# Softmax times V on one core: four heads loaded ahead in a fixed queue order, and a loop of 24 passes in place of the unrolled program

## The chip, the cores and the metric

The kernel runs on one core of a Trainium2 chip. The metric is the device time of one execution in microseconds (us), lower is better. A core has five engines that run their own instruction streams and meet through semaphores: TensorE (PE, with its weight loads shown apart as PEld), VectorE (DVE), ScalarE (ACT), GpSimd (POOL) and SyncE (SP). Here SP only issues DMA transfers. A transfer is spread over 16 DMA engines, and all that SP issues stands in one queue (q1 in the profile).

## The reference

```python
"scores": np.random.randn(8, 12, 1024, 1024).astype(np.float32)
"v":      np.random.randn(8, 12, 1024, 64).astype(np.float32)

scores_max = np.max(scores, axis=-1, keepdims=True)
attn = np.exp(scores - scores_max)
attn = attn / (np.sum(attn, axis=-1, keepdims=True) + 1e-8)
return np.matmul(attn, v).astype(np.float32)
```

So there are 96 independent heads. Each has a 1024x1024 matrix of scores (4 MB), a softmax along its rows, and a product with a 1024x64 matrix v (256 KB), which gives a 1024x64 output (256 KB).

## The kernel before

The kernel handles the 96 heads one after the other. A head's 1024 query rows lie on 128 partitions, R = 8 rows on each: row r of partition p is query p*8 + r. Per head n it does this:

- SP issues the load of v (L100, 128x512 fp32) and that of the scores (L104, one transfer of 4 MB, 128x8192 fp32; for the last head alone four transfers of 1 MB). POOL converts v to fp16 beside a column of ones (`vones`, L107).
- For each r, ACT takes the exponential of two rows at a time (EB = 2, L113, four calls a head) from `s_nat` to `p_nat` in fp16. No maximum is subtracted. PE transposes the row's eight 128x128 blocks into `psT` (L117, eight weight loads and eight matmuls), and DVE copies `psT` to `pt` (L123).
- Two rows later (LAG = 2), `finish` multiplies `pt` with `vones` (L76, eight weight loads and eight matmuls, 65 columns: 64 of v and the sum of the row). After every four rows (G = 4) DVE takes the reciprocal of the sums (L87) and multiplies (L88) into `out_sb`. After the eighth row SP issues the head's store (L95).

The whole program is unrolled: PE alone has 24576 instructions, SP 288 transfers and waits. Buffers come from rotating pools (4 for the scores, 4 for v, 3 for the outputs, 5 for `psT`, 3 for `psO`). A scheduler decides the order on each engine from the order in which the code is written and from when a pool's buffer comes free. SP works strictly in its order: while one of its instructions waits, all behind it wait. Each transfer raises one of eight completion semaphores (DMAHW0 to DMAHW7, taken in turn), and a transfer also waits for the one that used its semaphore before, eight transfers back.

Of the kernel before, what the change touches and what calls it, by code (L numbers as in the profile page):

```python
# [1 line left out]

# [5 lines left out]

FP32 = mybir.dt.float32
FP16 = mybir.dt.float16  # L10
EXP = mybir.ActivationFunctionType.Exp


@with_exitstack
def kernel(
    ctx: ExitStack,
    tc: tile.TileContext,
    scores: bass.AP,
    v: bass.AP,
    out: bass.AP,  # L20
):
    nc = tc.nc
    P = 128

    B, H, SQ, SK = scores.shape
    Bv, Hv, SKv, D = v.shape
    assert (B, H, SK) == (Bv, Hv, SKv)
    BH = B * H
    assert SQ % P == 0 and SK % P == 0
    R = SQ // P  # L30
    C = SK // P
    M = D + 1
    EB = 2
    G = 4
    LAG = 2
    NV = 3

    sc_bh = scores.rearrange("b h (p r) j -> (b h) p r j", p=P)  # L40
    v_bh = v.rearrange("b h (p c) d -> (b h) p c d", p=P)
    out_bh = out.rearrange("b h (p r) d -> (b h) p r d", p=P)

    const_pool = ctx.enter_context(tc.tile_pool(name="const", bufs=1))
    s_pool = ctx.enter_context(tc.tile_pool(name="spool", bufs=4))
    p_pool = ctx.enter_context(tc.tile_pool(name="ppool", bufs=6))
    v_pool = ctx.enter_context(tc.tile_pool(name="vpool", bufs=4))
    pt_pool = ctx.enter_context(tc.tile_pool(name="ptpool", bufs=5))
    ob_pool = ctx.enter_context(tc.tile_pool(name="obpool", bufs=3))
    rc_pool = ctx.enter_context(tc.tile_pool(name="rcpool", bufs=4))  # L50
    psT_pool = ctx.enter_context(tc.tile_pool(name="psTp", bufs=5, space=bass.MemoryType.PSUM))
    psO_pool = ctx.enter_context(tc.tile_pool(name="psOp", bufs=3, space=bass.MemoryType.PSUM))

    ident32 = const_pool.tile([P, P], FP32, name="ident32")
    make_identity(nc, ident32)
    ident16 = const_pool.tile([P, P], FP16, name="ident16")
    nc.vector.tensor_copy(out=ident16[:], in_=ident32[:])  # L57


    vones_bufs = []  # L60
    for k in range(NV):
        vo = const_pool.tile([P, C, M], FP16, name=f"vones{k}")
        nc.vector.memset(vo[:, :, D : D + 1], 1.0)  # L63
        vones_bufs.append(vo)

    pending = []

    def finish(u):

        n, r, pt, st = u  # L70
        g = r % G
        if g == 0:
            st["psO"] = psO_pool.tile([P, G, M], FP32, tag="psO", name="psO")
        psO = st["psO"]
        for c in range(C):
            nc.tensor.matmul(  # L76
                out=psO[:, g, :],
                lhsT=pt[:, c * P : (c + 1) * P],
                rhs=st["vones"][:, c, :],
                start=(c == 0),  # L80
                stop=(c == C - 1),
            )
        if g == G - 1:
            if r == G - 1:
                st["out_sb"] = ob_pool.tile([P, R, D], FP32, tag="out_sb", name="out_sb")
            recip = rc_pool.tile([P, G, 1], FP32, tag="recip", name="recip")
            nc.vector.reciprocal(out=recip[:], in_=psO[:, :, D : D + 1])  # L87
            nc.vector.tensor_tensor(  # L88
                out=st["out_sb"][:, r - G + 1 : r + 1, :],
                in0=psO[:, :, 0:D],  # L90
                in1=recip[:].to_broadcast([P, G, D]),
                op=mybir.AluOpType.mult,
            )
        if r == R - 1:
            nc.sync.dma_start(out=out_bh[n], in_=st["out_sb"][:])  # L95

    for n in range(BH):
        last = n == BH - 1
        v_sb = v_pool.tile([P, C, D], FP32, tag="v_sb", name="v_sb")
        nc.sync.dma_start(out=v_sb[:], in_=v_bh[n])  # L100
        s_nat = s_pool.tile([P, R, SK], FP32, tag="s_nat", name="s_nat")
        step = EB if last else R
        for r in range(0, R, step):
            nc.sync.dma_start(out=s_nat[:, r : r + step, :], in_=sc_bh[n, :, r : r + step, :])  # L104

        vones = vones_bufs[n % NV]
        nc.gpsimd.tensor_copy(out=vones[:, :, 0:D], in_=v_sb[:])  # L107
        st = dict(vones=vones)

        for r in range(R):  # L110
            if r % EB == 0:
                p_nat = p_pool.tile([P, EB, SK], FP16, tag="p_nat", name="p_nat")
                nc.scalar.activation(out=p_nat[:], in_=s_nat[:, r : r + EB, :], func=EXP)  # L113
            p_row = p_nat[:, r % EB, :].rearrange("p (q c) -> p c q", c=C)
            psT = psT_pool.tile([P, SK], FP16, tag="psT", name="psT")
            for c in range(C):
                nc.tensor.transpose(  # L117
                    out=psT[:, c * P : (c + 1) * P],
                    in_=p_row[:, c, :],
                    identity=ident16[:],  # L120
                )
            pt = pt_pool.tile([P, SK], FP16, tag="pt", name="pt")
            nc.vector.tensor_copy(out=pt[:], in_=psT[:])  # L123
            pending.append((n, r, pt, st))
            if len(pending) > LAG:
                finish(pending.pop(0))
    while pending:
        finish(pending.pop(0))


# [1 line left out]
_INS = ['scores', 'v']  # L132
_OUTS = [((8, 12, 1024, 64), 'float32')]


# [23 lines left out]
```

## Time and profile before

| | |
|---|---|
| median of 17 runs | 1287.81 us (1283.03 to 1293.08) |
| the profiled execution | 1285.99 us |
| its span in the profile | 1284.2 us, so 1.8 us lie around it |
| instructions | 27588 |
| bytes moved by the kernel's queue | 453.00 MB |
| mean rate over the span | 354 GB/s |
| mean granted clock of TensorE | 0.763 |

The page gives for each engine the time that it was busy, then the span in 40 slices, the DMA queues, the chain of work that ended last, and the groups of instructions by line. In a table of stretches the columns are the stretch, its length, the busy time of PE, PEld, DVE, ACT and POOL with their instruction counts, the granted TensorE clock, the mean busy share of the 16 DMA engines, and the rate in GB/s. A DMA share above 1 means that packets overlapped on an engine. "SPq" is SP issuing transfers. A line of the waits names who waited, for whom, and then the sum in us, the number of waits and the longest one.

### The profile page before, as it was taken

What the parts mean: (1) busy time and instruction counts of PE and PEld (TensorE: products, weight loads), DVE (VectorE), ACT (ScalarE), POOL (GpSimd) and SP (SyncE); (2) the same over time, 40 slices, a digit from 0 to 9 for tenths busy, and PEclk for the clock granted to TensorE, in tenths of its full rate; (3) what the DMA queues carried; (4) which work ended last, traced back from release to release, by engine and by line L of the source; (5) the groups of instructions that cost most, each with busy time, mean ns of one, the idle gap of its engine ahead of it and who ended that gap; (6) DMA issues with size and microseconds to landing.
All of it is one profiled execution on the core that took longest, in us unless ns stands there. A gap on an engine that the chain in (4) does not pass through costs nothing.

```text
span 1284.2 us, 27588 instructions
## 1 busy us (share of the span) xinstructions
PE 801.2 (62%) x12288; PEld 763.4 (59%) x12288; DVE 619.5 (48%) x1156; ACT 704.8 (55%) x385; POOL 59.9 (5%) x102
## 2 busy tenths in 40 slices
PE   4666566665756666566665666656656665766657
PEld 4566566654656666566664656656556664656556
DVE  3445454454544544445453554545445454454545
ACT  4464565645646565465644655455555645646455
POOL 0000000000000000000000000000000000000000
PEclk9777777777777877777777777777777777777778
DMA  9898898888988889998988989989798898988986
GB/s 400 329 357 361 345 373 335 362 359 346 367 359 352 355 343 362 355 365 344 361 360 345 377 335 357 374 361 374 309 372 356 352 369 350 366 340 354 377 345 263
DMA packets 42023, 454.76 MB, mean 354 GB/s; under 512 B 4656, under 2 KB 4656, under 8 KB 29232
## 3 DMA queue, kind: packets, MB, share of 16 engines
q1 hardware_dynamic: 41904, 453.00, 87.9%
q8 instruction: 96, 1.57, 0.5%
q14 instruction: 23, 0.19, 0.0%
HBM read 427.82 MB, written 25.17 MB: 353 GB/s over the span
## 4 chain that ended last, share of the span: by engine, by line
DMA 54%; PE 21%; ACT 8%; DVE 8%; issue 6%; SPq 3%; ACTq 0%
DMA s_nat<-in_scores_dram 54%; PE psT L117 16%; ACT p_nat L113 8%; PE psO L76 5%; DVE pt L123 3%; DVE out_sb L88 3%; SPq L100 2%; DVE recip L87 1%; SPq L95 1%; SPq L104 0%; ACTq L113 0%
## 5 line engine op out<-in xcount | busy, mean ns | idle before, releaser
L113 ACT ACTIVATE p_nat<-s_nat 128x2048 f16<-128x2048 f32 x384 | 703.5, 1903 | 572.1 <-DMA s_nat<-in_scores_dram 556.8
L117 PE MATMUL psT<-ident,p_nat 128*128 128x128 f16 x6144 | 636.5, 269 | 439.2 <-ACT p_nat L113 438.8
L123 DVE COPY pt<-psT 128x1024 f16<-128x1024 f16 x768 | 528.9, 690 | 606.9 <-PE psT L117 595.1
L117 PEld LDWEIGHTS <-p_nat 128*128 128x128 f16 x6144 | 540.0, 156 | 464.7 <-ACT p_nat L113 455.3
L76 PE MATMUL psO<-vones,pt 128*128 128x65 f16 x6144 | 347.7, 206 | 39.9 <-DVE pt L123 39.9
L76 PEld LDWEIGHTS <-pt 128*128 128x128 f16 x6144 | 300.0, 108 | 52.0 <-DVE pt L123 52.0
L107 POOL CAST vones<-v_sb 128x512 f16<-128x512 f32 x96 | 59.2, 617 | 1204.3 <-DMA v_sb<-in_v_dram 1115.4
L88 DVE TENSOR_TENSOR out_sb<-psO,recip 128x256 f32<-128x256 f32 x192 | 80.6, 420 | 3.3
L87 DVE RECIPROCAL recip<-psO 128x4 f32<-128x4 f32 x192 | 34.1, 178 | 50.1 <-PE psO L76 50.1
L113 ACT ACT_TABLE_LOAD x1 | 1.3, 1283 | 0.7 <-PEq L143 0.7
L63 DVE MEMSET vones<- 128x8 f16 x3 | 0.1, 65 | 0.8 <-PEq L143 0.8
L57 DVE CAST ident<-ident 128x128 f16<-128x128 f32 x1 | 0.2, 227 | 0.4 <-POOL ident masks.py:199 0.4
masks.py:199 POOL TENSOR_SCALAR_AFFINE_SELECT ident<-ident 128x128 f32<-128x128 f32 x1 | 0.3, 292 | 0.1
masks.py:197 POOL MEMSET ident<- 128x128 f32 x1 | 0.2, 204 | 0.3 <-POOLq L143 0.3
L143 POOL MEMSET const-float32-0.0<- 128x1 f32 x1 | 0.1, 98 | 0.2 <-issue 0.2
L143 POOL MEMSET const-bfloat16-1.0<- 128x1 bf16 x1 | 0.1, 101 | 0.0
L143 POOL MEMSET const-uint8-127<- 128x1 uint8 x1 | 0.1, 101 | 0.0
L143 POOL MEMSET const-float32-1.0<- 128x1 f32 x1 | 0.1, 98 | 0.0
## 6 DMA issues: line engine op xcount, KB each, us to landing
s_nat<-in_scores_dram SPq DMA_DIRECT2D x95, 4096.0 KB, 13.9
v_sb<-in_v_dram SPq DMA_DIRECT2D x96, 256.0 KB, 3.0
out_dram<-out_sb SPq DMA_DIRECT2D x96, 256.0 KB, 2.6
s_nat<-in_scores_dram SPq DMA_DIRECT2D x4, 1024.0 KB, 8.1
```

What stands on the lines that cost most here:

```text
L57: nc.vector.tensor_copy(out=ident16[:], in_=ident32[:])
L63: nc.vector.memset(vo[:, :, D : D + 1], 1.0)
L76: nc.tensor.matmul(out=psO[:, g, :], lhsT=pt[:, c * P : (c + 1) * P], rhs=st["vones"][:, c, :], start=(c == 0), stop=(c == C - 1),)
L87: nc.vector.reciprocal(out=recip[:], in_=psO[:, :, D : D + 1])
L88: nc.vector.tensor_tensor(out=st["out_sb"][:, r - G + 1 : r + 1, :], in0=psO[:, :, 0:D], in1=recip[:].to_broadcast([P, G, D]), op=mybir.Al ...
L95: nc.sync.dma_start(out=out_bh[n], in_=st["out_sb"][:])
L100: nc.sync.dma_start(out=v_sb[:], in_=v_bh[n])
L107: nc.gpsimd.tensor_copy(out=vones[:, :, 0:D], in_=v_sb[:])
L113: nc.scalar.activation(out=p_nat[:], in_=s_nat[:, r : r + EB, :], func=EXP)
L117: nc.tensor.transpose(out=psT[:, c * P : (c + 1) * P], in_=p_row[:, c, :], identity=ident16[:],)
L123: nc.vector.tensor_copy(out=pt[:], in_=psT[:])
L143: nc = _bacc.Bacc("TRN2", target_bir_lowering=False, num_devices=1)
```

## The change

Two things are changed together.

1. The order on SP's queue is written out by hand. Four buffers for the scores, four for v and four for `vones` belong to the four heads of a pass (k = 0 to 3). The first four heads are loaded before the loop. After that, the load of head n + 4 stands where head n's eighth row has been started (its exponentials release the buffer), and head n's store stands behind it. `queue` ties each transfer to the one before it on SP. The score load of every fourth head is two transfers of 2 MB, and the splitting of the last head's load into four goes.
2. `tc.For_i(0, 96, 4, iteration_sync="reg_based")` makes a loop in hardware: each engine has the code of four heads once and runs it 24 times. Waits in the loop compare with a value in a register that grows from pass to pass; there is no barrier between passes. In the last pass the loads are skipped by a condition.

Around these, all buffers are named tiles that `take` hands out in turn: 8 for `p_nat` (6 before), 4 for `pt` (5), 4 for `out_sb` (3), 4 for `psT` (5), 4 for `psO` (3). The work on the data is the same, instruction by instruction.

```diff
-    NV = 3
+    AHEAD = 4
...
+    s_bufs = buffers(sb_pool, AHEAD, [P, R, SK], FP32, "s_nat")
+    v_bufs = buffers(sb_pool, AHEAD, [P, C, D], FP32, "v_sb")
+    p_bufs = buffers(sb_pool, 8, [P, EB, SK], FP16, "p_nat")
+    pt_bufs = buffers(sb_pool, 4, [P, SK], FP16, "pt")
+    out_bufs = buffers(sb_pool, 4, [P, R, D], FP32, "out_sb")
...
+    psT_bufs = buffers(ps_pool, 4, [P, SK], FP16, "psT")
+    psO_bufs = buffers(ps_pool, 4, [P, G, M], FP32, "psO")
...
+    def queue(dma):
+        if queued:
+            tc.add_manual_dep(dma.ins, queued[-1].ins.name, ..., reason="queue order")
+        queued.append(dma)
...
         if r == R - 1:
-            nc.sync.dma_start(out=out_bh[n], in_=st["out_sb"][:])
+            dma = nc.sync.dma_start(out=one(out_bh, n), in_=st["out_sb"][:])
...
+            queue(dma)
...
+    def load(k, n, step=R, **cond):
+        queue(nc.sync.dma_start(out=v_bufs[k][:], in_=one(v_bh, n), **cond))
         for r in range(0, R, step):
...
+    def load_next(k, n0):
+        n = (n0 + (AHEAD + k)) % BH
+        load(k, n, R if k < AHEAD - 1 else R // 2, cond=n0 < BH - AHEAD)
+
+    def heads(n0):
+        for k in range(AHEAD):
...
+                nc.vector.tensor_copy(out=pt[:], in_=psT[:])
+                if r == R - 1:
+                    load_next(k, n0)
+                pending.append((n0 + k, r, pt, st))
+                if len(pending) > LAG:
+                    finish(pending.pop(0))
+        while pending:
+            finish(pending.pop(0))
...
+    for k in range(AHEAD):
+        load(k, k)
+    with tc.For_i(0, BH, AHEAD, iteration_sync="reg_based") as n0:
+        queued.clear()
+        heads(n0)
```

How the orders differ, first on SP, the issuing engine. Before, in the steady part (out_dram is a store, v_sb and s_nat are loads):

```order
L95 DMA out_dram<-out_sb 128x512 [waits DVE_49] x2
L100 DMA v_sb<-in_v_dram 128x512 [waits DMAHW0_49]
L104 DMA s_nat<-in_scores_dram 128x8192 [waits DMAHW1_49]
L95 DMA out_dram<-out_sb 128x512 [waits DMAHW2_49,DVE_49]
L100 DMA v_sb<-in_v_dram 128x512 [waits DMAHW3_49,Pool_49]
L104 DMA s_nat<-in_scores_dram 128x8192 [waits DMAHW4_49,Activation_49]
```

Three heads are loaded ahead of these rows; so the loads of head 3 (the fourth) stand behind the stores of heads 0 and 1, and each later load of head n behind the store of head n - 2. Now, the first heads of a pass (the number at a name is the buffer's; ISA and REGISTER_ALU compute addresses and the values to wait for):

```order
L140 DMA v_sb_83<-in_v_dram 128x512 [waits DMAHW0_I-123_own,Pool_I-123_own,DMAHW0_49]
L143 ISA
L143 REGISTER_ALU
L143 DMA s_nat_79<-in_scores_dram 128x8192 [waits DMAHW1_I-123_own,Activation_I-123_own,DMAHW1_49]
L124 ISA
L124 DMA out_dram<-out_sb_99 128x512 [waits DMAHW2_I-123_own,DVE_I-123_own]
L140 ISA x2
L140 DMA v_sb_84<-in_v_dram 128x512 [waits DMAHW3_I-123_own,Pool_I-123_own,DMAHW2_49]
L143 ISA x2
L143 DMA s_nat_80<-in_scores_dram 128x8192 [waits DMAHW4_I-123_own,Activation_I-123_own,DMAHW3_49]
L124 ISA
L124 DMA out_dram<-out_sb_100 128x512 [waits DMAHW5_I-123_own,DVE_I-123_own]
```

The load of head n + 4 now stands ahead of the store of head n; the wait for DVE that stood ahead of the load of head n + 2 stands behind that of head n + 4.

Second, PE at the seam between the fourth and the fifth head. Before, the next head's transposes (L117) follow at once:

```order
L76 LDWEIGHTS pt
L76 MATMUL psO<-vones_89,pt 128x65
L117 LDWEIGHTS p_nat [waits Activation_49]
L117 MATMUL psT<-ident_87,p_nat 128x128 [waits PE_49]
L117 LDWEIGHTS p_nat
```

Now the pass ends there with a step of the counter and a branch back:

```order
L105 REGISTER_ALU
L105 LDWEIGHTS pt_98 [waits DVE_I-123_own]
L105 MATMUL psO_114<-vones_77,pt_98 128x65
...
L187 ISA
L187 COMPARE_AND_BRANCH
L187 UNCONDITIONAL_BRANCH [waits barrier_Pool_Activation_PE_DVE_SP_release]
```

PE's code is 1079 rows in place of 24578, of which 1074 (rows 4 to 1077) are the pass; the wait for a barrier in the last row stands behind the loop and is met once.

More of the change, by code (lines that the diff above doesn't have):

```diff
@@ L60 @@
     vones_bufs = []
-    for k in range(NV):
+    for k in range(AHEAD):
         vo = const_pool.tile([P, C, M], FP16, name=f"vones{k}")
@@ L64, with buffers, take, one @@
         vones_bufs.append(vo)
-    pending = []
+    def buffers(pool, count, shape, dtype, name):
+        return [pool.tile(shape, dtype, name=f"{name}{k}") for k in range(count)]
+    s_bufs = buffers(sb_pool, AHEAD, [P, R, SK], FP32, "s_nat")
[3 more added lines that the diff above has]
+    out_bufs = buffers(sb_pool, 4, [P, R, D], FP32, "out_sb")
+    rc_bufs = buffers(sb_pool, 4, [P, G, 1], FP32, "recip")
+    psT_bufs = buffers(ps_pool, 4, [P, SK], FP16, "psT")
+    psO_bufs = buffers(ps_pool, 4, [P, G, M], FP32, "psO")
+    turn = {}
+    def take(bufs):
+        k = turn.get(id(bufs), 0)
+        turn[id(bufs)] = k + 1
+        return bufs[k % len(bufs)]
+    pending = []
+    queued = []
+    def queue(dma):
+        if queued:
+            tc.add_manual_dep(
+                dma.ins,
+                queued[-1].ins.name,
+                mybir.DependencyInfo(mybir.DependencyClass.NoSync, mybir.DependencyReason.DATA),
+                reason="queue order",
+            )
+        queued.append(dma)
+    def one(bh, n):
+        return bh[bass.ds(n, 1)].rearrange("o p r d -> (o p) r d")
     def finish(u):
@@ L72, in finish @@
         if g == 0:
-            st["psO"] = psO_pool.tile([P, G, M], FP32, tag="psO", name="psO")
+            st["psO"] = take(psO_bufs)
         psO = st["psO"]
@@ L84, in finish @@
             if r == G - 1:
-                st["out_sb"] = ob_pool.tile([P, R, D], FP32, tag="out_sb", name="out_sb")
-            recip = rc_pool.tile([P, G, 1], FP32, tag="recip", name="recip")
+                st["out_sb"] = take(out_bufs)
+            recip = take(rc_bufs)
             nc.vector.reciprocal(out=recip[:], in_=psO[:, :, D : D + 1])
@@ L94, in finish @@
         if r == R - 1:
[L95 to L102, printed above, removed]
-        for r in range(0, R, step):
[L104 to L120, printed above, removed]
-                )
[L122 to L126, printed above, removed]
@@ L127, with apart @@
-    while pending:
-        finish(pending.pop(0))
+            dma = nc.sync.dma_start(out=one(out_bh, n), in_=st["out_sb"][:])
+            for other in stores:
+                apart(dma, other)
+                apart(other, dma)
+            apart(dma, dma)
+            stores.append(dma)
+            queue(dma)
+    stores = []
+    def apart(dma, other):
+        tc.declare_no_dep(
+            dma.ins, other.ins, across_iterations=True, reason="stores of two heads are disjoint"
+        )
@@ new lines, in heads @@
+    def heads(n0):
+        for k in range(AHEAD):
+            nc.gpsimd.tensor_copy(out=vones_bufs[k][:, :, 0:D], in_=v_bufs[k][:])
+            st = dict(vones=vones_bufs[k])
+            for r in range(R):
+                if r % EB == 0:
+                    p_nat = take(p_bufs)
+                    nc.scalar.activation(
+                        out=p_nat[:], in_=s_bufs[k][:, r : r + EB, :], func=EXP
+                    )
+                p_row = p_nat[:, r % EB, :].rearrange("p (q c) -> p c q", c=C)
+                psT = take(psT_bufs)
+                for c in range(C):
+                    nc.tensor.transpose(
+                        out=psT[:, c * P : (c + 1) * P],
+                        in_=p_row[:, c, :],
+                        identity=ident16[:],
+                    )
+                pt = take(pt_bufs)
+                nc.vector.tensor_copy(out=pt[:], in_=psT[:])
[6 more added lines that the diff above has]
+            finish(pending.pop(0))
@@ L132 @@
+    assert BH % AHEAD == 0 and BH >= 2 * AHEAD
+    for k in range(AHEAD):
+        load(k, k)
+    with tc.For_i(0, BH, AHEAD, iteration_sync="reg_based") as n0:
+        queued.clear()
+        heads(n0)
 _INS = ['scores', 'v']
```

16 lines of the change are left out of this document (8 added, 8 removed).

## The prediction, made before the changed kernel had run

> **What bounds the kernel now.** I read the page first: busy shares, the DMA slices, the queues and the chain.
>
> ```profile
> PE 801.2 (62%) x12288; PEld 763.4 (59%) x12288; DVE 619.5 (48%) x1156; ACT 704.8 (55%) x385; POOL 59.9 (5%) x102
> DMA  9898898888988889998988989989798898988986
> q1 hardware_dynamic: 41904, 453.00, 87.9%
> q8 instruction: 96, 1.57, 0.5%
> DMA 54%; PE 21%; ACT 8%; DVE 8%; issue 6%; SPq 3%; ACTq 0%
> ```
>
> No engine is busy for two thirds of the span, the transfers are near 0.9, and the chain alternates between transfers and compute. So neither is the bound by itself; a loop of both is. Who closes it stands in the waits, first the engines', then SP's own.
>
> ```profile
> ACT p_nat L113 <- DMA s_nat<-in_scores_dram: 556.8, 92, 11.5
> PE psT L117 <- ACT p_nat L113: 438.8, 114, 15.5
> ```
>
> ```profile
> SPq L95 <- DVE out_sb L88: 1114.9, 96, 21.6
> SPq L104 <- ACT p_nat L113: 2.4, 7, 0.5
> ```
>
> ACT waits for scores, PE for ACT, but SP waits 1114.9 us for finished outputs, in front of its stores, and only 2.4 us for a free score buffer. The loads are late because they queue behind a store that waits. One turn of the loop, from the chain in the middle of the run:
>
> ```profile
> 582.56 0.43 DVE out_sb L88
> ...
> 583.01 0.34 SPq L95
> ...
> 583.45 0.38 SPq L100
> ...
> 583.92 14.00 DMA s_nat<-in_scores_dram
> ...
> 598.02 1.92 ACT p_nat L113
> ...
> 608.96 0.44 DVE out_sb L88
> ...
> 609.41 0.34 SPq L95
> ```
>
> A head's last output lets its store go at 583.01, the load of the head after next follows at 583.92 and lands 14.00 later, its compute takes until 609.41. That is 26.40 us for two heads, 13.2 a head; 96 of them make 1267 of the 1284.2. What the transfers could do, and what they do, is in a table of stretches:
>
> ```profile
> 4.00:14.00 10.00, 0.00 (x0) 0.00 (x0) 0.00 (x0) 0.49 (x1) 0.26 (x1) 1.00 1.04 446
> 14.00:24.00 10.00, 8.16 (x120) 7.91 (x120) 5.85 (x10) 6.94 (x5) 0.62 (x1) 1.00 1.02 435
> 2.80:34.10 31.30, 16.11 (x248) 15.47 (x248) 11.98 (x22) 14.66 (x8) 1.84 (x3) 0.95 1.00 424
> 36.80:38.00 1.20, 0.00 (x0) 0.00 (x0) 0.00 (x0) 1.07 (x1) 0.00 (x0) 0.80 1.22 387
> 596.20:597.80 1.60, 0.00 (x0) 0.00 (x0) 0.00 (x0) 0.00 (x0) 0.00 (x0) 0.85 0.68 225
> 60.00:1260.00 1200.00, 753.63 (x11557) 718.17 (x11553) 582.27 (x1083) 659.50 (x360) 55.51 (x90) 0.76 0.89 356
> ```
>
> While three loads stood in the queue at the start, it moved 424 GB/s over 31.3 us at a share of 1.00, with PE, DVE and ACT at work in two thirds of it. Later it averages 356, and between one load's end and the next one's start (596.20 to 597.80) it falls to 225.
>
> **The change, part by part.**
>
> *Order of the queue.* The load of head n + 4 now waits for ACT's last exponential of head n and no longer for an output. It also waits for its completion semaphore's last user, eight transfers back: followed through SP's rows, v of head n + 4 waits at the worst for the store of n - 2, which lies behind the scores of n + 2. So it is issued when n + 2 has landed and n + 3, 11 us of transfer, has still to run. How long an issue takes to reach the engines is seen at the start of the chain:
>
> ```profile
> 0.74 0.39 SPq L100
> ...
> 3.07 33.75 DMA s_nat<-in_scores_dram
> ```
>
> The first load is issued at 0.74, and the full stretch of the table begins at 2.80: 2.1 us, which the 11 cover. The queue should not run dry. What waits behind SP's wait: the store of n, whose output is done long before, and the next load, with the 11 us as cover. If that cover went, the gaps of today would be back (priced under the rivals).
>
> So the time is that of the bytes: 453.00 MB / 424 GB/s = 1068 us, 11.13 a head, 44.5 a pass. The ends: at the 446 of the best ten microseconds 1016; if each packet took as long as now, 0.879 x 1284.2 = 1129. I take 1068: packets are long now where a queue starts from empty (1.22 share for 387 GB/s at 36.80), and a queue that is kept full resembles the first stretch. That stretch has no finished stores in it; they are in the bytes at 0.62 us each, and the 36.80 row, where a store and a load mix, gives 0.68 at its 387, 6 us more in all.
>
> *Engines under it.* What each needs for a head must stay under 11.13.
>
> ```profile
> L113 ACT ACTIVATE p_nat<-s_nat 128x2048 f16<-128x2048 f32 x384 | 703.5, 1903 | 572.1 <-DMA s_nat<-in_scores_dram 556.8
> L113 ACT ACT_TABLE_LOAD x1 | 1.3, 1283 | 0.7 <-PEq L143 0.7
> L95 SPq EVENT_SEMAPHORE  x94: 17/17/17, 36.9 to 1274.1; - x94
> ```
>
> ```profile
> 599.99 2.88 PE L117 MATMUL psT<-ident,p_nat 128*128 128x128 f16 x24 [5.74 <-ACT p_nat L113]
> 602.66 0.65 PE L76 MATMUL psO<-vones,pt 128*128 128x65 f16 x8
> 608.27 0.43 PE L76 MATMUL psO<-vones,pt 128*128 128x65 f16 x8 [0.41 <-DVE pt L123]
> ```
>
> ACT: 4 x 1.903 = 7.6, and the table load, which is now in the pass, 1.283 / 4 = 0.3: 7.9. PE: from 599.99 to 608.70, 8.7. DVE: 619.5 / 96 = 6.5. POOL 0.6. All are covered; slack of PE, the tightest, 4 x (11.13 - 8.7) = 9.7 us a pass.
>
> *The loop.* Per pass PE has 48 more small register instructions (1074 rows less 1024 and the two of the branch), DVE as many, ACT and SP fewer. Nothing in the trace is like them: below, 17 ns as for SP's semaphore event, 0.8 us a pass; above, 0.34 as for SP issuing a store, 16 us a pass, which would make PE the bound at 51 us. I take the lower, since neither moves data. The branch itself is bounded by nothing and by the 9.7 us of slack; under that it costs nothing, as four heads' buffers lie ahead and no barrier holds SP. All else (p_nat 8, pt 4, psT 4, psO 4) changes at most PE's waits inside that slack.
>
> *Instruction blocks.* q8 is PE's code: 24576 instructions in 96 blocks, 256 instructions and 16 KB each, 0.5% of 16 x 1284.2, so 1.07 us each. They share the 16 engines, and a load counts as landed only when its last engine is done. The queues from 24 to 37 us, and one stretch:
>
> ```profile
> q8 instruction: 2, 0.03, 1.0%
> ```
>
> ```profile
> 35.20:36.40 1.20, 0.00 (x0) 0.00 (x0) 0.31 (x1) 0.00 (x0) 0.00 (x0) 1.00 0.09 36
> ```
>
> The third load, issued at 3.07 in the row above, landed 33.75 later, at 36.82, though from 35.20 on a share of 0.09 was busy, little more than one engine of 16. Two blocks fell into those 13 us: they made one engine 2.7 us later than the others, 1.35 each. In the steady state of today the gaps between loads let that engine catch up. In a full queue nothing does: every block fetched puts 1.35 us on the path. The pass has 1074 PE rows, 4.2 blocks. If PE keeps them, q8 goes silent after the first pass, and this costs some 5 x 1.35 = 7 us, hidden in the start. No row tells which, since now each instruction runs once. I take that it keeps them, narrowly.
>
> [...]
>
> *Ends.* Start 2.8. Five stores come after the last load: 453.00 - 5 x 0.26 = 451.69 MB, 1065 us. Tail:
>
> ```profile
> 1275.75 1.91 ACT L113 ACTIVATE p_nat<-s_nat 128x2048 f16<-128x2048 f32 x1 [2.04 <-DMA s_nat<-in_scores_dram]
> ```
>
> From this last exponential to the end it took 8.45; the last piece is now 2 MB, not 1, one call more: 10.4.
>
> Sum: 2.8 + 1065 + 10.4 = 1078 of span, 1080 with the 1.8 us around it. The profiled execution (1285.99) lies 1.8 below the median (1287.81), so 1082.
>
> [...]
>
> **The rivals.** "Faster" and "slower" mean by over 0.2%, about what a measurement here can tell from no change.
>
> 1. *The blocks keep coming.* PE fetches its pass anew after each branch, four or five blocks: 44.5 + 4 x 1.35 = 49.9 to 51.3 a pass, x 24 = 1198 to 1230, with the ends and the 3.6 between span and median 1215 to 1247. For it: q8 brings one block per 256 instructions all through; against: 4.2 blocks need little room. Chance 0.27.
> 2. *Slower: the branch refills more than the pass holds.* Same place, but blocks are fetched that the branch then throws away. It breaks even where 24 x (44.5 + x) + 17 = 1288, x = 8.5 us, so 6.3 blocks a pass. [...] Against it: now 96 blocks serve 24576 instructions, so none is fetched for nothing. Chance 0.07.
> 3. *PE becomes the bound.* The clock at the start of a burst is low:
>
> ```profile
> 600.00:604.00 4.00, 4.00 (x41) 3.88 (x42) 2.08 (x3) 4.00 (x3) 0.00 (x0) 0.50 1.01 434
> ```
>
> At 0.50 a transpose takes 2.88 / 24 = 0.120, a product 0.65 / 8 = 0.081; 64 of each are 12.9 us, above 11.13: 96 x 12.9 + 17 = 1255. Against it: PE's gaps get shorter, not longer, and later in each burst it is faster (0.43 for eight). The upper price of the register instructions would end near here too. Chance 0.05.
> 4. *No change.* Either the 356 GB/s of the long stretch is what memory sustains, 453.00 / 356 = 1272 + 17 = 1289, or the semaphores hold each load until the queue is empty, and the gap of today, 13.2 - 11.13 = 2.1 us a head, stays: 1285. Against the first: 424 to 446 in whole loads; against the second: the 11 us above. Chance 0.05.
>
> **How the numbers follow.** The forecast has 0.54, its own range 1050 to 1145: below, between 424 and 446 GB/s (1016 + 17 = 1033 and the sum's 1082), above, the 1129 of unchanged packets and 17. Rival 1 0.27, rival 2 0.07, rival 3 0.05, rival 4 0.05; 0.02 for slower by a cause not named. The range of 1050 to 1250 takes in the forecast, rival 1 and half of rival 3, and leaves out less than 2 in 10. Faster: 0.54 + 0.27 + 0.05 = 0.86; of rival 4 I give all to the same, 0.05; slower 0.07 + 0.02 = 0.09.
>
> **What would show it.** Right: DMA slices of 9 throughout at about 420 GB/s; SP's wait for DVE nearly gone, replaced by waits for transfers or ACT; the chain nearly all transfers of scores; q8 with some 10 blocks or fewer. Rival 1: q8 near 96 to 120, the DMA share near 0.9 with ACT waiting for scores. [...] Rival 3: PE's waits for ACT gone, its clock near 0.5. Rival 4: slices as today. I would be wrong above all if PE's code does not stay where it is.

## The result, and the profile after

| | before | after |
|---|---|---|
| median | 1287.09 us (47 runs) | 1072.29 us (8 runs, 1071.13 to 1072.8) |
| the profiled execution, its span | 1285.99, 1284.2 | 1071.92, 1070.1 |
| mean rate over the span | 354 GB/s | 423 GB/s |

The ratio is 0.8331, with a 95% interval of 0.8317 to 0.8345: 215 us less. Ratios are taken over fast runs: of the four runs of the kernel below with v in eight buffers, one of 1762.94 us is a slow one that its median in the table counts, and the other three took 1133.98 to 1138.96. The lines of the page that answer to those shown of before:

```profile
PE 754.1 (70%) x12288; PEld 713.0 (67%) x12288; DVE 610.7 (57%) x1157; ACT 733.7 (69%) x408; POOL 59.9 (6%) x102
DMA  9999999999999999999999999999999999999995
q1 hardware_dynamic: 44784, 453.00, 99.7%
q8 instruction: 3, 0.05, 0.0%
DMA 69%; PE 8%; PEld 8%; DVE 5%; ACT 4%; SPq 3%; issue 2%; ACTq 0%
```

Every slice but the last is a 9, and the packets of q1 took 99.7% of 16 engines' span. The chain is not nearly all transfers, as the prediction had said it would be: they are 69% of it. PE's code came in three blocks, not 96. The engines did the same work in less time, so their shares rise, yet none is near full.

The waits, the engines' and then SP's own:

```profile
ACT p_nat L163 <- DMA s_nat<-in_scores_dram: 156.9, 50, 7.6
PE psT L169 <- ACT p_nat L163: 266.0, 73, 15.6
```

```profile
SPq L124 <- DMA s_nat<-in_scores_dram: 291.7, 46, 8.9
SPq L140 <- DMA s_nat<-in_scores_dram: 239.0, 46, 6.5
SPq L140 <- DMA out_dram<-out_sb: 236.4, 23, 10.3
SPq L124 <- DVE out_sb L117: 26.3, 9, 8.7
```

SP waited 1114.9 us for outputs; now 26.3. What it waits for is older transfers: each transfer waits for the last one that had its semaphore. By the semaphores that the trace names, that one is always eight transfers back in the kernel before; of the 13 transfers of a pass here it is eight back for five, five back for five and 13 back for three. The 23 waits for a store, one a pass, are those that the prediction had followed: v of head n + 4 for the store of n - 2. Such waits are harmless here, since they end while the scores of one to three loads, whole or half, still stand in the queue: when a load of v is issued after one, 8.4 us of transfer or more have still to run by the ninth of the 16 completion events. Three links of the chain of waits, one a pass:

```profile
489.37 29.63 DMA s_nat<-in_scores_dram
...
533.30 29.68 DMA s_nat<-in_scores_dram
...
577.29 29.62 DMA s_nat<-in_scores_dram
```

They start 43.9 and 44.0 us apart: a pass of four heads, 10.99 a head, where a head took 13.2. Each spends 29.6 us in the queue, behind others, against 14.00 before; that is what a full queue looks like. The long stretch, which was read at 356 GB/s before (there up to 1260):

```profile
60.00:1060.00 1000.00, 717.18 (x11692) 678.47 (x11693) 579.94 (x1095) 699.57 (x390) 55.49 (x90) 0.83 1.01 428
```

428 GB/s over 1000 us, at a share of 1.01.

### The profile page after: what moved, and what is told of

Its sections match the earlier page's. It is cut to its first block, busy times and chain, and to the rows that moved or that the text cites. A ratio compares the mean times of both kernels' runs of the same rounds, so it can differ in the third digit from the quotient of the medians.

```text
span 1070.1 us, 31933 instructions
## 1 busy us (share of the span) xinstructions
PE 754.1 (70%) x12288; PEld 713.0 (67%) x12288; DVE 610.7 (57%) x1157; ACT 733.7 (69%) x408; POOL 59.9 (6%) x102
## 2 busy tenths in 40 slices
DMA packets 44787, 453.05 MB, mean 423 GB/s; under 512 B 4976, under 2 KB 4976, under 8 KB 29552
## 3 DMA queue, kind: packets, MB, share of 16 engines
q1 hardware_dynamic: 44784, 453.00, 99.7%
## 4 chain that ended last, share of the span: by engine, by line
DMA 69%; PE 8%; PEld 8%; DVE 5%; ACT 4%; SPq 3%; issue 2%; ACTq 0%
DMA s_nat<-in_scores_dram 67%; PEld L169 6%; PE psT L169 6%; DVE pt L175 4%; ACT p_nat L163 4%; DMA out_dram<-out_sb 3%; PE psO L105 3%; PEld L105 2%; SPq L140 2%; SPq L143 1%; SPq L124 0%; DVE recip L116 0%; ACTq L163 0%; DVE out_sb L117 0%
## 5 line engine op out<-in xcount | busy, mean ns | idle before, releaser
L175 DVE COPY pt<-psT 128x1024 f16<-128x1024 f16 x768 | 516.4, 690 | 432.3 <-PE L169 213.9
L169 PE MATMUL psT<-ident,p_nat 128*128 128x128 f16 x6144 | 571.1, 251 | 266.6 <-ACT p_nat L163 266.0
L169 PEld LDWEIGHTS <-p_nat 128*128 128x128 f16 x6144 | 494.4, 153 | 281.5 <-ACT p_nat L163 277.1
L105 PE MATMUL psO<-vones,pt 128*128 128x65 f16 x6144 | 375.0, 205 | 44.7 <-DVE pt L175 38.1
L105 PEld LDWEIGHTS <-pt 128*128 128x128 f16 x6144 | 305.5, 106 | 70.9 <-DVE pt L175 68.8
L163 ACT ACT_TABLE_LOAD x24 | 30.8, 1283 | 168.2 <-DMA s_nat<-in_scores_dram 163.4
L117 DVE TENSOR_TENSOR out_sb<-psO,recip 128x256 f32<-128x256 f32 x192 | 81.0, 422 | 4.9
```

Source lines behind the costliest of these rows:

```text
L105: nc.tensor.matmul(out=psO[:, g, :], lhsT=pt[:, c * P : (c + 1) * P], rhs=st["vones"][:, c, :], start=(c == 0), stop=(c == C - 1),)
L117: nc.vector.tensor_tensor(out=st["out_sb"][:, r - G + 1 : r + 1, :], in0=psO[:, :, 0:D], in1=recip[:].to_broadcast([P, G, D]), op=mybir.Al ...
L163: nc.scalar.activation(out=p_nat[:], in_=s_bufs[k][:, r : r + EB, :], func=EXP)
L169: nc.tensor.transpose(out=psT[:, c * P : (c + 1) * P], in_=p_row[:, c, :], identity=ident16[:],)
```

## The experiments

Each kernel ran beside the kernel before on the same chip, and the ratios are to that. Two kernels of this table are compared by their ratios and spans.

| kernel | median, us | ratio to before (95%) |
|---|---|---|
| changed kernel | 1072.29 | 0.8331 (0.8317 to 0.8345) |
| order alone, unrolled | 1085.44 | 0.8449 (0.8427 to 0.8472) |
| loop alone, first form | 1403.54 | 1.0922 (1.0867 to 1.0976) |
| loop alone, order of before on every engine | 1335.03 | 1.039 (1.0354 to 1.0426) |
| eight heads a pass | 1140.24 | 0.8878 (0.8853 to 0.8902) |
| eight heads, v in eight buffers | 1136.75 | 0.8858 (0.8821 to 0.8895) |
| the same, whole score loads | 1093.02 | 0.8526 (0.8488 to 0.8563) |
| store ahead of the load | 1073.32 | 0.8355 (0.8332 to 0.8377) |
| last loads in pieces | 1071.49 | 0.8351 (0.833 to 0.8371) |
| two score buffers | 1113.86 | 0.8685 (0.8651 to 0.8719) |

**The order alone.** The loop is taken away, the queue's order stays.

```diff
-    with tc.For_i(0, BH, AHEAD, iteration_sync="reg_based") as n0:
-        queued.clear()
+    for n0 in range(0, BH, AHEAD):
         heads(n0)
```

> The new queue order alone: the same loads ahead and the same stores, but the program is unrolled over 96 heads, without the loop. Theory (two parts, each needed): the queue stays full, so PE's code blocks, one per 256 instructions, fall on one DMA engine that never catches up. The full queue of the changed kernel takes 10.98 us a head; with 1.35 us per block 12.33 a head, 96 x 12.33 + 16 for the ends = 1200 us, with blocks of 1.07 us 1173. q8 shows 96 blocks, the DMA share is near 0.92, and ACT waits for scores whose other 15 engines are long done. Rival (the order does it all, the loop only shortens the code): 1072 to 1080 us, DMA slices of 9.

Measured: 1085.44 us, far below the 1173 that my theory allowed. The page:

```profile
DMA  9999999999999999999999999999999999999993
q1 hardware_dynamic: 44784, 453.00, 98.6%
q8 instruction: 96, 1.57, 0.5%
```

So the order brings nearly all of the gain, and the loop the last 13 us, 1.2%. All 96 blocks of code came, but they did not cost 1.35 us each on the path. Each transfer leaves 16 completion events in the trace (4976 for the 311 transfers of the changed kernel), read here as one of each of the 16 DMA engines, and these show why. The first engine to finish keeps the pace of the changed kernel: it ends the last scores at 1054.6 in both. The others fall behind it and do not catch up: the ninth of the 16 is 0.2 us late at the first transfer of scores, 2.6 at the 25th, 5.2 at the 49th, 11.9 at the 97th and 14.5 at the last, and the last engine, for which a load must wait (in the changed kernel ACT starts on the last piece 0.11 us after the last event), is 18.0 late. In the changed kernel the median stays 0.2 behind throughout, and the last engine 2.6 after the three blocks of the first pass. The slowest engine's delay grows in some eleven steps of 1.2 to 1.5 us. So the 1.35 is about what a block costs the engine that it falls on; but the 96 fell on several engines in turn, not on one (on about nine of the 16, an estimate from 96 blocks and the eleven steps), and a load waits only for the worst of these. The last scores end at 1072.3 there against 1056.9, 15.4 later; what comes behind them is 1.0 shorter, and that is the 14.4 us between the spans (1084.5 and 1070.1).

**The loop alone.** Four heads a pass, but each head's scores are loaded behind the store of two heads earlier, as before.

```diff
         if r == R - 1:
             ...
             queue(dma)
+            load_next(st["k"], st["n0"])
...
-        n = (n0 + (AHEAD + k)) % BH
+        n = (n0 + (2 + k)) % BH
...
-                if r == R - 1:
-                    load_next(k, n0)
```

> The loop alone: 24 passes over four heads, but SP's order is that of the kernel before (the load of head n + 2 stands behind the store of head n), and each head is finished before the next one starts on PE; two of the four casts to vones run on DVE. Theory: the loop of transfer and compute comes back, with gaps in the queue, but each load now lands without the delay from a code block, which the trace of before shows as 1.25 us between the median and the last of 16 engines: 13.2 - 1.25 / 2 = 12.6 a head to 13.2 - 1.25 = 11.95, so 1165 to 1225 us. Rival (today's gaps hide the blocks): 1275 to 1295 us, as before. Rival (the loop does it all): 1072.

Measured: 1403.54 us. It missed theory and rivals, and it is no clean test: inside the pass the scheduler had put the next head's transposes ahead of the last products of the head, so that a store, and with it a load, waited for the scores of the next head; and half of the conversions of v ran on DVE, not POOL. SP's wait shows the lengthened loop:

```profile
SPq L124 <- DVE out_sb L117: 1177.3, 96, 24.1
```

The second form ties the first transposes of a head behind the last product of the head before on PE and DVE, and leaves the conversion on POOL. From the kernel before it still differs in v, which is loaded four heads ahead, in the half loads of every fourth head, and in the numbers of buffers.

> The loop alone, now with the kernel before's order on all engines: on SP the scores of head n + 2 stand behind the store of head n (v, with four buffers, is loaded for n + 4 there), all casts stay on POOL, and on PE and DVE a head is finished before the next one's transposes. The first try at this let PE's order interleave two heads, so that a store waited for the next head's scores. Theory: the loop of transfer and compute is that of the kernel before, and without code blocks a load lands up to 1.25 us earlier: 1200 to 1285 us, well below the 1403 of the first try. Rival (the loop's waits and branches lengthen each turn): 1330 us or more.

Measured: 1335.03 us, 3.9% slower than before, at the lower end of what the rival said and outside the theory's range. SP's wait, and one turn of the chain:

```profile
SPq L134 <- DVE out_sb L127: 1102.5, 96, 20.6
```

```profile
606.51 0.44 DVE out_sb L127
606.96 0.36 SPq L134
...
607.75 0.33 SPq L151
...
608.52 14.81 DMA s_nat<-in_scores_dram
...
623.88 0.84 issue
624.72 1.92 ACT p_nat L179
...
636.40 0.43 DVE out_sb L127
636.85 0.35 SPq L134
```

This turn for two heads is 29.89 us, 606.96 to 636.85, where it was 26.40. It is a long one, with a table load between landing and first exponential (next line). From issues and completion events of heads 4 to 91, a turn takes 27.74 us on average, and 26.61 before. Of the 1.13 us, 0.45 lie between the issue of the store and that of the scores (1.55 for 1.10), where SP now also computes addresses and the values to wait for. The other 0.68 lie between the issue of the scores and the next store. There the first head of a pass waits 1.38 us from landing to first exponential, for 0.10 before, and the three heads whose scores come whole take 12.0 us from first exponential to store, for 11.6. The transfer of a whole load takes 12.6 to 16.5 us by its place in the pass, 13.7 to 14.0 before, so the 14.81 of this turn tells little.

```profile
623.43 1.28 ACT L179 ACT_TABLE_LOAD   x1 [13.59 <-DMA s_nat<-in_scores_dram]
```

That is ACT's timeline. So the loop is not free; in the changed kernel its cost does not show, since there the queue stays full all the same.

**Eight heads a pass.** Does PE keep any pass, or only one that is small enough? 2151 rows on PE in place of 1079.

```diff
-        for k in range(AHEAD):
+        for k in range(2 * AHEAD):
...
-    with tc.For_i(0, BH, AHEAD, iteration_sync="reg_based") as n0:
+    with tc.For_i(0, BH, 2 * AHEAD, iteration_sync="reg_based") as n0:
```

> The changed kernel with eight heads in a pass and 12 passes; the same four buffers and the same queue order; four of the eight casts to vones run on DVE. PE's code is 2151 rows in place of 1079. [...]

Measured: 1140.24 us, with four of the eight conversions of v on DVE. q8 was 107 blocks, so PE did not keep this pass. The second form has v in eight buffers and all conversions on POOL.

> Eight heads in a pass again, now with all casts on POOL; v has eight buffers and is loaded eight heads ahead, the scores four heads ahead as in the changed kernel. In the first try a cast on DVE waited up to 21.8 us for a v that was not yet loaded. Theory: PE's 2151 rows do not stay, q8 shows some 107 blocks as in the first try, and they cost what they cost in the unrolled order, 13 us: 1080 to 1092 us. Rival (a pass that does not stay also stalls PE at the branch, and that was the loss): 1110 us or more.

Measured: 1136.75 us. The number is the rival's, but not by the rival's cause, as SP's rows show. The page, SP's wait, two rows of SP's timeline, and the stretch around the second:

```profile
q1 hardware_dynamic: 44784, 453.00, 95.8%
q8 instruction: 107, 1.75, 0.6%
```

```profile
SPq L140 <- DMA s_nat<-in_scores_dram: 486.9, 48, 22.1
```

```profile
207.96 0.36 SPq L124 DMA_DIRECT2D out_dram<-out_sb  x1
230.57 0.34 SPq L140 DMA_DIRECT2D v_sb<-in_v_dram  x1
```

```profile
228.00:234.00 6.00, 5.23 (x100) 4.77 (x96) 5.02 (x11) 6.00 (x4) 0.62 (x1) 1.00 0.63 217
```

Once in a pass, eleven times, SP issues nothing for 21.5 to 23.1 us, here until the last score piece that it had issued has landed (230.46); then the queue is empty, and six microseconds move 217 GB/s. A pass has 26 transfers, and the eight semaphores are given out anew from the first in each pass (so they are in the changed kernel's trace, where of the loop's eight five tell of 46 or 47 transfers and three of 23 or 24). Since 26 is not a multiple of eight, the first v load of a pass gets the semaphore of a piece that was issued only two transfers before it, at 198.67; the trace's completion events name the same semaphore for both. With the 13 transfers of the changed kernel the first v load follows its semaphore's last user, a store, by five transfers, and by the last completion event 10.9 us of transfer are still queued when it goes. To try the cause, every score load was made whole, 24 transfers a pass:

```diff
-        step = R if k % AHEAD < AHEAD - 1 else R // 2
+        step = R
```

> The pass of eight heads again, with v in eight buffers, but every head's scores in one transfer: 24 transfers a pass in place of 26. Open is why the pass of eight heads took 1136.75 us. Theory: once in a pass the first v load waits 22 us on SP for a score load, since the transfers' completion semaphores are given in a ring that starts anew with each pass, and 26 is not a multiple of eight, so this v gets the semaphore of a load that was only just issued; the queue then runs dry for some 4 us, twelve times. With 24 the ring goes on in turn: the wait of about 22 us before a v load is gone, q1 is back near 99%, and the time is 1072 + 13 (107 code blocks, as in the unrolled kernel) + about 3 (a last piece of 4 MB in place of 2): 1083 to 1095 us. Rival: PE, or another engine, stalls at the branch where its code is fetched anew, and the wait of SP only shows it: the time stays at 1125 to 1140 whatever the number of transfers. q8 stays at about 107 blocks by both.

Measured: 1093.02 us, inside the theory's 1083 to 1095. The page and SP's wait:

```profile
DMA  9999999999999999999999999999999999999982
q1 hardware_dynamic: 41472, 453.00, 98.0%
q8 instruction: 107, 1.75, 0.6%
```

```profile
SPq L140 <- DMA s_nat<-in_scores_dram: 610.8, 94, 10.4
```

The longest of these waits is 10.4 us, and the queue stays full. What is left above the changed kernel lies at the end of the scores, 1074.0 against 1056.9 (107 blocks of code: the last DMA engine is 19.0 us behind the first by then), and in the 3.5 us that the time behind a last load of 4 MB is longer. PE's branch at the end of a pass, first in the changed kernel, then with eight heads and 26 transfers (each row: count, then minimum, median and maximum in ns, and the first and last start):

```profile
L187 PEldq COMPARE_BRANCH  x25: 88/223/238, 1.3 to 1065.2; - x25
```

```profile
L193 PEldq COMPARE_BRANCH  x13: 88/3412/4352, 1.3 to 1127.1; - x13
```

With 1074 rows the branch takes 0.22 us. With 2151 it takes 3.4, and nine blocks come in every pass (107 over 12). Eleven times 3.4 us are 37, close to the 41.9 between the spans with 26 and 24 transfers (1132.6 and 1090.7), so it has to be told apart from SP's wait. PE's own timeline does that: the branch ahead of the gap shown began at 194.2 and ended at 198.0, and PE's next transposes still had to wait for ACT:

```profile
200.28 2.89 PE L173 MATMUL psT<-ident,p_nat 128*128 128x128 f16 x24 [5.79 <-ACT p_nat L167]
```

The branch lay inside that wait, and so it was at each of the eleven: PE's next weight load starts 0.05 us after ACT's first exponential of the pass ends, 1.4 to 3.4 us after the branch's end. SP's wait ended with a landing. Against the 428 GB/s of a full queue, six microseconds around the end of each of the eleven waits lose 36 us in all. With 24 transfers the same branch has a median of 0.57 us; why it is shorter there was not tried.

**Store ahead of the load.** Head n's store stands in front of the load of n + 4, not behind it.

> The changed kernel with the load of head n + 4 behind the store of head n, not ahead of it; all else the same. Theory (what counts is how much work stands in the queue when a load is issued, not which of the two stands first): the store of n goes when head n + 1 has been begun, some 6 us after it landed; n + 2 and n + 3 still have about 16 us to run, so the queue stays full: 1070 to 1080 us. Rival (a load behind a store that waits is the cause of the gaps, whatever the distance): the gap comes back at least in part, 1150 us or more.

Measured: 1073.32 us, no difference from the changed kernel. The page and SP's wait:

```profile
q1 hardware_dynamic: 44784, 453.00, 99.5%
```

```profile
SPq L124 <- DVE out_sb L117: 169.4, 50, 24.4
```

SP waits for DVE for 169.4 us again, with loads behind the waiting store, and nothing is lost: when a store is issued, the transfers queued ahead of it still have 10.9 us or more to run, by their completion events. So with loads four heads ahead it does not count which of the two comes first; how much is queued while SP waits does.

**Two score buffers.** The load of n + 2 is released by the exponentials of n, with v four ahead as in the changed kernel.

```diff
-    s_bufs = buffers(sb_pool, AHEAD, [P, R, SK], FP32, "s_nat")
+    s_bufs = buffers(sb_pool, 2, [P, R, SK], FP32, "s_nat")
...
+        load_s(k, (n0 + (2 + k)) % BH, step, **(cond if k >= 2 else {}))
```

> The changed kernel with two score buffers in place of four: the load of head n + 2 is released by ACT's last exponential of head n and stands ahead of the store of n. Theory (what counts is the work in the queue when a load is issued): it is issued some 8 us after n landed, when n + 1 has about 3 us to run; an issue needs 2.1 us, so the queue just stays full or nearly so: 1075 to 1140 us. Rival (the four heads ahead are what the gain needs): 1200 us or more.

Measured: 1113.86 us, inside the theory's range. With half the buffers four fifths of the gain remain (1284 to 1114, against 1072). SP's waits:

```profile
SPq L124 <- DVE out_sb L117: 509.1, 96, 8.5
SPq L145 <- ACT p_nat L167: 341.8, 58, 15.2
```

SP now waits for ACT to free a buffer, 341.8 us where it was 2.4 in the kernel before, with at most one head's scores left in the queue (2.1 to 11.2 us of them), and a head takes (1112.9 - 16) / 96 = 11.4 us rather than 10.98, if start and end take 16 us as in the changed kernel. Here the place in the queue does count: the second form of the loop alone has the scores two heads ahead as well, but behind the store, and took 1335.03.

**The last loads in pieces.** The third head's scores of a pass come in two transfers and the fourth's in four.

```diff
-        load(k, n, R if k < AHEAD - 1 else R // 2, cond=n0 < BH - AHEAD)
+        load(k, n, (R, R, R // 2, R // 4)[k], cond=n0 < BH - AHEAD)
```

> The changed kernel with the scores of the third head of a pass in two transfers and of the fourth in four (one and two before). Theory: the bytes and the full queue are as before, but in the tail ACT can start on the last two heads' rows before they have landed whole; ACT works without a gap from 1046.3 to 1061.0 there, and of this 2 to 6 us go: 1066 to 1070 us. Rival (the two more transfers a pass hold up the queue by their semaphores): 1072 us or more, with DMA slices below 9.

Measured: 1071.49 us, no gain that can be told from none, and the theory's 1066 to 1070 missed. ACT's rows at the end, first in the changed kernel, then with the pieces:

```profile
1046.33 14.71 ACT L163 ACTIVATE p_nat<-s_nat 128x2048 f16<-128x2048 f32 x8 [3.61 <-DMA s_nat<-in_scores_dram]
```

```profile
1038.15 16.68 ACT L163 ACTIVATE p_nat<-s_nat 128x2048 f16<-128x2048 f32 x9 [2.37 <-DMA s_nat<-in_scores_dram]
1055.37 1.91 ACT L163 ACTIVATE p_nat<-s_nat 128x2048 f16<-128x2048 f32 x1 [0.54 <-PE psO L105]
1057.81 1.91 ACT L163 ACTIVATE p_nat<-s_nat 128x2048 f16<-128x2048 f32 x1 [0.53 <-PE L169]
1060.27 1.91 ACT L163 ACTIVATE p_nat<-s_nat 128x2048 f16<-128x2048 f32 x1 [0.55 <-PE psT L169]
```

The pieces do what they were meant to do: the last three exponentials each start 0.1 us behind the landing of a piece (completion events at 1055.26, 1057.71 and 1060.17; the rows put these waits down to PE), and from the end of the last scores to the end of the span it is 9.5 us, not 13.2. But the last scores end at 1059.8, not at 1056.9, and these 2.9 us take back most of the 3.7. So the same bytes took longer with 16 transfers a pass than with 13; whether by their number or by the smaller packets (q1 has 54720 in place of 44784; a load of 1 MB went in packets of 8 KB in the kernel before, and the changed kernel's q1 has none of that size) was not tried. No version tried is clearly faster than the changed kernel.

## Why the prediction was right, and where it was off

The prediction was 1082 us, 9.7 above the 1072.29 measured, and the forecast's own mechanism is the one that the runs show. Point by point:

- *The bound.* That the chain alternated between transfers and compute, closed by SP's wait for outputs in front of a store, is shown: the new order alone takes the time to 1085.44, and the old order in the loop gives 1335.03. But the new order changes two things, the place of a load (ahead of the store) and its distance (four heads ahead, not two). Against that 1335.03, whose kernel also ties the order on PE and DVE, the distance alone gives 1073.32 (store ahead of the load) and the place alone 1113.86 (two score buffers). The prediction did not part them.
- *The queue stays full.* Right. I had 11 us of work queued when a load is issued; by the completion events of the median engine the scores of a head are issued between 6.9 and 24 us before the scores ahead of them have landed, at worst less than the 11, and still above the 2.1 of an issue.
- *The term of the bytes.* Mis-sized. I took 424 GB/s from the first 31 us, 11.13 a head; it was 428 over the long stretch, 10.99 a head by the chain. The last scores ended at 1056.9, not at 1067.8 (2.8 + 1065). That is 10.9 of the difference.
- *The tail.* Mis-sized the other way: 13.2 us from the last scores to the end of the span, not 10.4. ACT took the last piece as it landed (first exponential at 1057.33, completion event 1057.22). But PE was behind: after eight exponentials without a break (the row at 1046.33 above, which ends at 1061.04) its last transposes start 1.60 us after the last exponential's end. In the kernel before, where ACT had paused for the last piece, they start 0.05 us after it (1275.75 + 1.91). Another 0.6 us lie between the last output and the end of the program (3.8 for 3.2). Bytes and tail together make 8.1 of span, 1070.1 for 1078; the rest is that the profiled run was 0.4, not 1.8, off the median. So the two errors stood against each other, and part of the closeness of the number is luck. The rows of these transposes, before and after:

```profile
1277.71 1.21 PE L117 MATMUL psT<-ident,p_nat 128*128 128x128 f16 x16 [1.43 <-ACT p_nat L113]
```

```profile
1062.64 1.19 PE L169 MATMUL psT<-ident,p_nat 128*128 128x128 f16 x16
```

- *Engines and loop.* The pass's code was covered, as predicted. A register instruction on PE took 32 to 37 ns, twice the 17 that I took and a tenth of the upper bound, and the branch 0.22 us; the table load, 24 x 1.28 = 30.8 us, was covered by ACT's slack. I costed the loop at nothing under that cover, and this holds only under it: with the old order it lost 3.9%.
- *Instruction blocks.* That PE keeps a pass of 4.2 blocks was the step that I held narrowly, and it is right: three blocks in the span, with 24 branches at the end of a pass. With 2151 rows nine came in every pass; no pass between the two was tried. Rival 1's price, 1.35 us on the path per block, was wrong by a factor of about ten, so its 1215 to 1247 would hardly have come even if PE had fetched anew: 96 blocks cost 13 us (unrolled), and a loop that does fetch anew, nine blocks a pass, gave 1093.02. The step that failed there is "every block fetched puts 1.35 us on the path", read from two blocks at the start of the run. A block does hold up its engine by about that much (1.2 to 1.5 us), and in a full queue the engine does not catch up; but over the run several engines took turns, by the estimate above about nine. I gave a quarter of the chances, and the upper half of the range, to a mechanism that I had priced from that one place.
- *Rivals 3 and 4.* PE's granted clock rose to 0.84, not toward 0.50, and PE waits 266.0 us for ACT. 428 GB/s is sustained, so the 356 of before was the queue, not memory.

## What to carry to other kernels

Look at what stands in front of a load on the issuing engine: a store that waits for compute makes every load behind it wait for that compute (SP's waits for outputs were 1114.9 us before and are 26.3 now). There are two ways out, and here either brought most of the gain: issue the load several heads ahead, so that the queue outlasts the wait (1073.32 us), or put it in front of the store, where its buffer comes free (1113.86 us). Judge a queue by the microseconds of transfer left in it when an issue waits, not by the wait itself: 169.4 us of waits lost nothing where 10.9 us or more were queued. The loop was worth its cost (issue arithmetic, a table load of 1.28 us in each pass) with a full queue and the 1074 rows that PE kept: it brought the last 13 us. With 26 transfers in a pass of eight heads a load shared a semaphore with one just issued, and most of 41.9 us went there; on a path of latencies the loop lost 3.9%.

## What the runs showed of the hardware

- A block of PE's code of 16 KB took one DMA engine a median of 0.96 us in the kernel before and 0.89 to 0.96 us in the changed one. With the queue full and the program unrolled, the delay of the slowest engine grew in steps of 1.2 to 1.5 us, and the late engines did not catch up. The engine changes over the run: 96 blocks made eight of the 16 engines 14.5 us late or more and the last one 18.0, and cost the kernel 13 us, not 96 times a block.
- The completion semaphores start anew in each pass of the loop: in the changed kernel's trace, 13 transfers a pass, five of the eight come up twice a pass and three once. With 26 transfers a pass that was a wait of 22 us on SP and a gap in the queue, eleven times, and most of 41.9 us; with 24 it is gone. That the ring is the cause rests on these two runs and on the events, by which the waiting load and the piece that ends its wait have one semaphore; the semaphores themselves were not changed by hand. The changed kernel has 13 a pass and loses nothing, so not every such number hurts.
- The mean granted clock of TensorE rose from 0.763 to 0.84, with PE busy for 70% of the span in place of 62%. Why was not tried.
